# Small constants ahead of the weights, scan rows 521 wide, a pad at SBUF's right end: every large tile at a multiple of 256 bytes

## The chip, the cores and the metric

One core of a Trainium2 chip runs one decoder layer. The metric is device time of one execution, in microseconds (us), lower is better. The kernel before was timed in three runs: 2541.51, 2540.04 and 2535.76 us, median 2540.04. One more execution was recorded by the hardware profiler.

Engines: PE is TensorE (matmuls), PEld its load of the stationary operand, DVE is VectorE, ACT ScalarE, POOL GpSimd, SP the engine that issues most DMAs. SBUF is the working memory, 128 partitions wide; PSUM takes what PE writes.

## The reference

A layer for 2048 tokens of width 1024, in float32:

```
a = rmsnorm(x);  u = a @ W_in                       # 1024 x 2560
conv = swish(layernorm(depthwise_conv31(val * sigmoid(gate))))   # 512 channels
attn = per head: A[t,s] = sigmoid(z_ts) * prod_{s<j<t} (1 - sigmoid(z_tj)),  out = A @ v
h = x + rmsnorm(concat(conv, rmsnorm(attn)) @ W_out)
out = h + rmsnorm((silu(f @ W_gate) * (f @ W_up)) @ W_down),  f = rmsnorm(h),  hidden 2816
```

The attention has 8 heads of 64, no softmax: the product over the keys between is a running product, swept in blocks.

## The kernel before, in words

**Products.** Each float32 matrix product is made of three PE products in the type fp32r: every operand is split in a rounded part H and a rest L, and L·H, H·H and H·L are summed in PSUM. A PE product has a stationary operand of 128x128 (512 bytes a partition, loaded for every product by an instruction of its own) and a moving operand of 128x512 (2048 bytes a partition). In the names of the profile, `out<-moving,stationary`. `dense` (L251 to L260) is this for the input projection, `product` (L1017) for the block products of the feed-forward stage, `slot` (L1332) for the last product, both through the helper `matmul` (L763). There are also transposes: 128x128 products with the identity `idr` as the moving operand, such as L590.

**Stages.** A table (`PLAN`, L39) runs the input projections (L256 to L260), output projections (L689 to L691) and the first feed-forward products (names `c` and `p`) of four groups of 512 tokens one after the other. Beside them, at places that another table sets, run attention (`scores` L555, `values` L581), the 31 conv taps on DVE and sums of weights on POOL. When these are through (about 1520 us into the span) the feed-forward stage proper follows: `five` (L1099), a loop over 44 blocks of five products (names `b<-...`), and then the product with `w_down`, a loop over 154 `slots` (L1325; names `dps<-...`), which ends the kernel. On PE the order of both is written out in the program; it is not changed.

**Where tiles lie.** SBUF tiles come from pools. A pool takes the next free bytes of each partition from the left end (or, with `side="right"`, from the right end), in the order in which the pools are opened; a tile starts at a multiple of 32 bytes. So the place of every large tile follows from the sizes of the small ones that lie before it. The pools, from the left: `consts` (identity, vectors), `weights` (wH, wL, raw), `rows` (L145: rows of 1024, pieces of 512), `small` (L146: some 40 tiles of 4 to 64 bytes), `mixconsts` (L276: conv weights, layernorm vectors, mask), `acts` (L277: xH, xL), `sums`, `conv`, and then `attn` (L281: QH, QL, K, V, om, A, TH, TL) whose space the pool `late` (tiles e0 to e5) takes over in the feed-forward stage. From the right: `mixed` (L275), whose space `ffnt` (tiles t0 to t3) takes over. `om` (L567) holds a row of 512 factors and one more column, 513 in all, for the running product (L573).

Start addresses modulo 256, as the built programs have them:

| tiles | role on PE | before | after |
|---|---|---|---|
| idr | moving in transposes | 128 | 128 |
| wH, wL, and `a22h` in `rows` | stationary in most products, moving in the output projection | 64 | 0 |
| xH, xL | moving in most products; stationary in the output projection; both in `dps` | 192 | 0 |
| QH, QL, K, V | K moving, QH and QL stationary (L563, L564); V stationary (L595, L596) | 192 | 0 |
| A; TH, TL | stationary in transposes; moving (L595, L596) | 64 | 0 |
| e0 to e5 | moving in `five` | 192 | 0 |
| t0 to t3 | moving in `five` (second half) | 224 | 0 |
| om, four buffers | not read by PE | 192, 224, 0, 32 | 0, 64, 128, 192 |

PE reads slices of these tiles at steps of 512 or 2048 bytes, so a slice has the residue of its tile.

Of the kernel before, what the change touches and what calls it, by code (L numbers as in the profile page):

```python
# [9 lines left out]
F32 = mybir.dt.float32  # L10
# [8 lines left out]
P = 128  # L19
# [9 lines left out]
G = 512  # L29
# [6 lines left out]
NOM = 4  # L36
# [102 lines left out]
def layer_kernel(ctx: ExitStack, tc: tile.TileContext, x, xT, g_pre_mix, w_in, conv_w, conv_b, ln_g, ln_b,  # L139
                 attn_g, w_out, g_post_mix, g_pre_ffn, w_gate, w_up, w_down, g_post_ffn, out):  # L140
    nc = tc.nc
    cp = ctx.enter_context(tc.tile_pool(name="consts", bufs=1))
    dp = ctx.enter_context(tc.tile_pool(name="scratch", bufs=1, space=DRAM))
    wp = ctx.enter_context(tc.tile_pool(name="weights", bufs=2))
    rp = ctx.enter_context(tc.tile_pool(name="rows", bufs=3))  # L145
    sp = ctx.enter_context(tc.tile_pool(name="small", bufs=2))  # L146
    mm = ctx.enter_context(tc.tile_pool(name="mm", bufs=2, space=PSUM))

    idr = cp.tile([P, P], F32R, name="idr")
# [34 lines left out]
        nc.sync.dma_start(t, src.partition_broadcast(P))  # L184
        return t

    def rstd_of(dst, ss, n, tag="ms"):

        w = dst.shape[-1]
        m = sp.tile([P, 8], F32, tag=tag, name=tag, bufs=4)  # L190
        nc.gpsimd.tensor_scalar(m[:, 0:w], ss, 1.0 / n, EPS, ALU.mult, ALU.add)
        nc.gpsimd.tensor_tensor(dst, m[:, 0:w], nhalf[:, 0:w], ALU.pow)

    def rms_of(dst, src, junk=None):

        ss = sp.tile([P, 1], F32, tag="ss", name="ss", bufs=4)
        nc.scalar.activation(ev("junk", BF16, D) if junk is None else junk, src, AF.Square, accum_out=ss)
        rstd_of(dst, ss, D)
# [73 lines left out]

    A = ExitStack()
    M = ExitStack()
    cm = M.enter_context(tc.tile_pool(name="mixed", bufs=1, side="right"))  # L275
    cc = ctx.enter_context(tc.tile_pool(name="mixconsts", bufs=1))  # L276
    xp = ctx.enter_context(tc.tile_pool(name="acts", bufs=1))  # L277
    C = ExitStack()
    fup = C.enter_context(tc.tile_pool(name="sums", bufs=1))
# [1 line left out]
    ap = A.enter_context(tc.tile_pool(name="attn", bufs=2))  # L281
# [201 lines left out]
    def convnorm(g, acc):  # L483

        for t in range(TT):
            ts_ = slice(t * P, (t + 1) * P)
            ps = pp.tile([P, G], F32, tag="cv", name="lps", bufs=1)
            for c in range(CB):
                nc.tensor.transpose(ps[:, c * P:(c + 1) * P], acc[:, c, ts_], id32)
            y = vp.tile([P, CH], F32, tag="cy", name="cy", bufs=1)  # L490
            nc.scalar.activation(y, ps, AF.Copy)
            st = sp.tile([P, 6], F32, tag="st", name="st")
            nc.vector.bn_stats(st, y)
            mv = sp.tile([P, 3], F32, tag="mv", name="mv")
            nc.vector.bn_aggr(mv[:, 0:2], st)
            rstd_of(mv[:, 2:3], mv[:, 1:2], 1, "msc")
            nc.vector.scalar_tensor_tensor(y, y, mv[:, 0:1], lng, ALU.subtract, ALU.mult)
            nc.vector.scalar_tensor_tensor(y, y, mv[:, 2:3], lnb, ALU.mult, ALU.add)
            s = vp.tile([P, CH], F32, tag="cs", name="cs", bufs=1)
            nc.scalar.activation(s, y, AF.Sigmoid)  # L500
            nc.gpsimd.tensor_tensor(s, y, s, ALU.mult)
            for _ in range(LAG):
                yield 3
            pt = pp.tile([P, G], F32, tag="cv", name="cps", bufs=1).rearrange("p (c t) -> p c t", c=CB)
            for c in range(CB):
                nc.tensor.transpose(pt[:, c, :], s[:, c * P:(c + 1) * P], id32)
            r = s.rearrange("p (c t) -> p c t", c=CB)
            nc.scalar.activation(r, pt, AF.Copy)
            nc.scalar.dma_start(conv[g][:, :, ts_], r)
        done.add(("conv", g))  # L510
# [23 lines left out]
    def attn(g):  # L534
# [20 lines left out]
        def scores(u, j):  # L555
            hd_ = heads[u["h"]]
            diag = u["c"] == g
            w = (j + 1) * P if diag else G
            K = u["K"]
            z = pp.tile([P, G], F32, tag="z", name="z")  # L560
            late = g == NG - 1 and u["h"] >= NH // 2
            js = slice(j * P, (j + 1) * P)
            nc.tensor.matmul(z[:, 0:w], hd_["QL"][:, js], K[:, 0:w], start=True, stop=False)  # L563
            nc.tensor.matmul(z[:, 0:w], hd_["QH"][:, js], K[:, 0:w], start=False, stop=True)  # L564
            if diag:
                nc.vector.tensor_tensor(z[:, w - P:w], z[:, w - P:w], msk, ALU.add)  # L566
            om = ap.tile([P, G + 1], F32, tag="om", name="om", bufs=NOM)  # L567
            nc.gpsimd.tensor_copy(om[:, G:G + 1], hd_["prev"][j])
            nc.scalar.activation(om[:, G - w:G], z[:, 0:w], AF.Sigmoid, scale=-0.125)  # L569
            a = ap.tile([P, G], F32, tag="A", name="A", bufs=NA)  # L570
            nc.scalar.activation(a[:, 0:w], z[:, 0:w], AF.Sigmoid, scale=0.125)  # L571
            r = om[:, G - w:G + 1][:, ::-1]
            nc.vector.tensor_tensor_scan(r, r, (one if late else z[:, 0:1]).to_broadcast([P, w + 1]), one, ALU.mult, ALU.bypass)  # L573
            nc.gpsimd.tensor_tensor(a[:, 0:w], a[:, 0:w], om[:, G - w + 1:G + 1], ALU.mult)  # L574
            pv = sp.tile([P, 1], F32, tag="pv", name="pv", bufs=8)
            nc.gpsimd.tensor_copy(pv, om[:, G - w:G - w + 1])
            hd_["prev"][j] = pv
            u["A"].append(a)
            return w
# [295 lines left out]
    def input_sums(g, k, tmp, banks=bank, t4=None):  # L875

        def turn(k, name):
            ps = banks(name)
            for t in range(TT):
                nc.tensor.transpose(ps[:, t * P:(t + 1) * P], rows["h", (g + 1) * TT + t][:, k * P:(k + 1) * P], id32)  # L880
            return ps

        def piece(k, i):
            t = ev("piece")
            nc.sync.dma_start(t, stored["fx", g, k, i])
            return t

        def halves(n, t):
            if n == 4 and t4:
                sums_split(t4, k, t)  # L890
            else:
                part(t, k, TT, "B", g, n)

        lo, hi = gpf[:, k:k + 1], gpf[:, k + 4:k + 5]
        t1, b22, t3, t2 = tmp
        p12, p22 = turn(k, "b12"), turn(k + 4, "b22")
        b11, b21 = piece(k, 0), piece(k, 1)
        nc.scalar.activation(b22, p22, AF.Copy, scale=hi)
        yield
        nc.vector.scalar_tensor_tensor(t1, p12, lo, b11, mult, sub)  # L900
        nc.vector.scalar_tensor_tensor(t3, p12, lo, b22, mult, sub)
        nc.gpsimd.tensor_tensor(t1, t1, b21, sub)
        halves(3, b22)
        halves(7, t3)
        yield
        nc.gpsimd.tensor_tensor(t2, b22, t1, sub)
        halves(5, t1)
        halves(6, t2)
        t, b21 = piece(k + 4, 0), piece(k + 4, 1)
        yield  # L910
        nc.vector.tensor_tensor(t, t, t2, sub)
        nc.vector.tensor_tensor(t, t, b21, add)
        halves(4, t)
        yield
# [39 lines left out]
    for name, g, cost, *mid in PLAN:  # L954
# [14 lines left out]
        n = 0  # L969
# [15 lines left out]
    with ExitStack() as E:  # L985
# [247 lines left out]
        def steps():  # L1233
# [10 lines left out]
            for k in range(TT):  # L1244
                yield from input_sums(last, k, tmp, bank, B[last][4])
            M.close()
            R.append(ctx.enter_context(tc.tile_pool(name="ffnt", bufs=1, side="right", reuse_waits="tile")))
# [40 lines left out]
        ss = {}  # L1288
# [8 lines left out]
        def scale_of(T, c):  # L1297

            if c:
                return scales.pop(T)  # L1300
            ms = sp.tile([P, 1], F32, tag="msf", name="msf", bufs=4)
            g, q = T // (2 * TT), T % (2 * TT)
            nc.gpsimd.tensor_scalar(ms, ss[g][:, 0, q:q + 1], ss[g][:, 1, q:q + 1], EPS, add, add)  # L1303
            rs = sp.tile([P, 1], F32, tag="rs", name="rs", bufs=4)
            nc.gpsimd.tensor_tensor(rs, ms, nhalf[:, 0:1], ALU.pow)  # L1305
            scales[T] = rs
            return rs
# [3 lines left out]
        def finish(T, r, t, c):  # L1311
            rs = scale_of(T, c)
            cs_ = slice(c * G, (c + 1) * G)
            tc.keep_in_program_order(
                nc.vector.scalar_tensor_tensor(r[:, cs_], t, rs, r[:, cs_], mult, add))
# [131 lines left out]
```

## Time and profile before

| | |
|---|---|
| timed runs, median | 2540.04 us (2535.76 to 2541.51) |
| span of the profiled execution, first to last instruction | 2537.7 us |
| busy: PE, DVE, POOL, ACT | 95%, 71%, 60%, 51% |
| mean granted PE clock | 0.983 |
| DMA, mean | 259 GB/s |

The record lists no other time of the profiled execution; its span lies inside the range of the three runs. PE's busy time is an envelope: a 128x512 product is listed with some 390 ns from its start to its modelled end, but the next one starts well before that end. How fast PE goes is therefore read from the spacing of starts: the number of products in a stretch in which PE never stops. Each row of the view by stretches gives, for every engine, its busy time and in brackets its number of instructions.

### The profile page before, as it was taken

How to read it: one execution, taken by the hardware profiler on the slowest of the kernel's cores; microseconds unless marked ns; L12 is line 12 of the kernel's file. 1: busy time of each engine (PE TensorE's matmuls, PEld its weight loads, DVE VectorE, ACT ScalarE, POOL GpSimd, SP SyncE). 2: the span in 40 equal slices, each digit the busy share in tenths (PEclk: the TensorE clock that was granted, in tenths of full speed). 3: DMA queues.
4: the chain of work that ended last, by engine and by line, in shares of the span. 5: the costliest groups of instructions: out<-in, count | busy, mean ns of one | idle time of the engine just before them, and what ended most of it. 6: DMA issues, size and time to landing. Idle time of an engine off the chain costs nothing. (4 is left out here: it accounts for less than half of the span.)

```text
span 2537.7 us, 35647 instructions
## 1 busy us (share of the span) xinstructions
PE 2417.8 (95%) x11156; PEld 1952.5 (77%) x11156; DVE 1806.6 (71%) x2321; ACT 1292.9 (51%) x2398; POOL 1518.9 (60%) x1844
## 2 busy tenths in 40 slices
PE   7989989998899999999989999999999999999998
PEld 6878767776677877888778877777788888887886
DVE  5787579887899787777887536776666665557656
ACT  4554655646565565666667645332332224444443
POOL 5754678646563376646745408764665665558656
PEclk9989999999899999999999999999999999999999
DMA  9979987987576699765786686977878768667765
GB/s 346 318 271 320 298 256 257 366 273 253 180 269 218 193 305 335 242 229 187 242 279 216 217 293 226 342 277 244 306 276 274 261 224 300 196 194 262 251 188 178
DMA packets 289181, 657.31 MB, mean 259 GB/s; under 512 B 33888, under 2 KB 42080, under 8 KB 288992
## 3 DMA queue, kind: packets, MB, share of 16 engines
q1 hardware_dynamic: 264704, 622.01, 73.6%
q10 hardware_dynamic: 24288, 33.04, 3.6%
q8 instruction: 88, 1.44, 0.2%
q14 instruction: 101, 0.83, 0.1%
HBM read 460.92 MB, written 193.99 MB: 258 GB/s over the span
## 5 line engine op out<-in xcount | busy, mean ns | idle before, releaser
L574 POOL TENSOR_TENSOR A<-A,om 128x512 f32<-128x512 f32 (+2 forms) x320 | 320.5, 1003 | 322.1 <-DVE om L573 242.9
L1054 POOL TENSOR_TENSOR wL<-raw,wH 128x512 fp32r<-128x512 f32 x176 | 255.7, 1477 | 204.9 <-ACT wH L1053 197.1
L476 DVE SCALAR_TENSOR_TENSOR cv<-glu,cw,cv 128x512 f32<-128x512 f32 x464 | 346.5, 747 | 5.7
L573 DVE TENSOR_TENSOR_SCAN om<-om,one,z 128x513 f32<-128x513 f32 (+3 forms) x256 | 277.5, 1097 | 73.9 <-ACT A L571 65.5
L1285 DVE TENSOR_TENSOR xL__22005<-t__22007,xH__22004 128x512 fp32r<-128x512 f32 x154 | 198.9, 1297 | 158.7 <-ACT xH__22004 L1284 158.4
L1283 POOL TENSOR_TENSOR xL__22003<-t__22006,xH__22002 128x512 fp32r<-128x512 f32 x154 | 212.4, 1386 | 154.3 <-ACT xH__22002 L1282 151.9
L256 PE MATMUL inps<-xH,wL 128*128 128x512 f32 x640 | 262.1, 410 | 6.7 <-ACT sg L422 5.0
L569 ACT ACTIVATE om<-z 128x512 f32<-128x512 f32 (+2 forms) x320 | 171.6, 537 | 181.2 <-DVE z L566 76.0
L258 PE MATMUL inps<-xH,wH 128*128 128x512 f32 x640 | 258.4, 404 | 0.0
L260 PE MATMUL inps<-xL,wH 128*128 128x512 f32 x640 | 258.3, 405 | 0.0
L249 DVE TENSOR_TENSOR TL<-at,TH 128x512 fp32r<-128x512 f32 (+1 forms) x320 | 189.0, 598 | 92.6 <-ACT TH L248 91.7
L763 PE MATMUL dps<-xH__22002,xL__22005 128*128 128x512 f32 x616 | 240.3, 390 | 2.8 <-DVE xL__22005 L1285 1.5
L763 PE MATMUL dps<-xL__22003,xH__22004 128*128 128x512 f32 x616 | 240.2, 390 | 1.0 <-POOL xL__22003 L1283 1.0
L763 PE MATMUL dps<-xH__22002,xH__22004 128*128 128x512 f32 x616 | 239.8, 389 | 0.0
L248 ACT ACTIVATE TH<-at 128x512 fp32r<-128x512 f32 (+1 forms) x320 | 167.6, 545 | 86.8 <-PE at L590 84.0
L1282 ACT ACTIVATE xH__22002<-t__22006 128x512 fp32r<-128x512 f32 x154 | 97.2, 631 | 215.4 <-POOL xL__22003 L1283 121.8
L590 PE MATMUL at<-idr,A 128*128 128x128 f32 x1088 | 189.5, 278 | 5.7 <-POOL A L574 4.7
L210 ACT ACTIVATE wH<-raw 128x1024 fp32r<-128x1024 f32 x156 | 165.6, 1063 | 41.7 <-DMA raw<-in_w_in_dram 24.4
L571 ACT ACTIVATE A<-z 128x512 f32<-128x512 f32 (+2 forms) x320 | 167.8, 539 | 33.3 <-PE at L590 33.3
L1053 ACT ACTIVATE wH<-raw 128x512 fp32r<-128x512 f32 x176 | 101.2, 623 | 153.7 <-PE b L763 51.0
L590 PEld LDWEIGHTS at<-idr,A 128*128 128x128 f32 x1088 | 140.6, 143 | 43.3 <-POOL A L574 6.6
L847 POOL TENSOR_TENSOR sum<-sum 128x512 f32<-128x512 f32 x88 | 114.2, 1297 | 84.7 <-DMA sum<-in_w_up_dram 37.8
(303 smaller groups left out, 6378.9 us busy)
## 6 DMA issues: line engine op xcount, KB each, us to landing
wL<-wL SPq DMA_DIRECT2D x156, 512.0 KB, 4.8
raw<-in_w_in_dram SPq DMA_DIRECT2D x80, 512.0 KB, 6.0
t__22007<-u SPq DMA_DIRECT2D x154, 256.0 KB, 3.0
c<-c ACTq DMA_DIRECT2D x88, 256.0 KB, 4.2
t__22006<-wd SPq DMA_DIRECT2D x88, 256.0 KB, 3.0
K<-kd SPq DMA_DIRECT2D x80, 256.0 KB, 4.7
V<-vd SPq DMA_DIRECT2D x80, 256.0 KB, 4.1
u<-accf SPq DMA_DIRECT2D x22, 768.0 KB, 4.2
```

The source lines that it names most:

```text
L249: nc.vector.tensor_tensor(L, ps, H.bitcast(F32), ALU.subtract)
L256: nc.tensor.matmul(ps, WL[:, kc], aH[t](k), start=k == 0, stop=False)
L258: nc.tensor.matmul(ps, WH[:, kc], aH[t](k), start=False, stop=False)
L260: nc.tensor.matmul(ps, WH[:, kc], aL[t](k), start=False, stop=k == KT - 1)
L476: nc.vector.scalar_tensor_tensor(to, gl[c][:, k:k + G], cw[:, c, k:k + 1], a, ALU.mult, ALU.add))
L573: nc.vector.tensor_tensor_scan(r, r, (one if late else z[:, 0:1]).to_broadcast([P, w + 1]), one, ALU.mult, ALU.bypass)
L574: nc.gpsimd.tensor_tensor(a[:, 0:w], a[:, 0:w], om[:, G - w + 1:G + 1], ALU.mult)
L590: nc.tensor.transpose(pt[:, j * P:(j + 1) * P], u["A"][j][:, b * P:(b + 1) * P], id32)
L763: return nc.tensor.matmul(ps, a, b, skip_group_check=True, **flags)
L1054: nc.gpsimd.tensor_tensor(l, t, f32(h), sub)
L1283: nc.gpsimd.tensor_tensor(WL, w, f32(WH), sub)
L1285: nc.vector.tensor_tensor(UL, t, f32(UH), sub)
```

## The change

Four things are done to places in SBUF, and nothing to what is computed. The pools `mixconsts` and `small` are opened ahead of `weights`. A tile `edge` of 224 bytes is put at the right end, and POOL clears it. `om` is 521 columns wide instead of 513. Two tags of small tiles are made smaller: `msc` has two buffers instead of four, and the tile `msf` of the last stage takes over the buffers of `msa`, which the attention used.

```diff
     cp = ctx.enter_context(tc.tile_pool(name="consts", bufs=1))
     dp = ctx.enter_context(tc.tile_pool(name="scratch", bufs=1, space=DRAM))
+    cc = ctx.enter_context(tc.tile_pool(name="mixconsts", bufs=1))
+    sp = ctx.enter_context(tc.tile_pool(name="small", bufs=2))
     wp = ctx.enter_context(tc.tile_pool(name="weights", bufs=2))
     rp = ctx.enter_context(tc.tile_pool(name="rows", bufs=3))
-    sp = ctx.enter_context(tc.tile_pool(name="small", bufs=2))
...
-    def rstd_of(dst, ss, n, tag="ms"):
+    def rstd_of(dst, ss, n, tag="ms", bufs=4):
...
-        m = sp.tile([P, 8], F32, tag=tag, name=tag, bufs=4)
+        m = sp.tile([P, 8], F32, tag=tag, name=tag, bufs=bufs)
...
+    edge = ctx.enter_context(tc.tile_pool(name="edge", bufs=1, side="right"))
+    nc.gpsimd.memset(edge.tile([P, 56], F32, name="edge"), 0.0)
     cm = M.enter_context(tc.tile_pool(name="mixed", bufs=1, side="right"))
-    cc = ctx.enter_context(tc.tile_pool(name="mixconsts", bufs=1))
...
-            rstd_of(mv[:, 2:3], mv[:, 1:2], 1, "msc")
+            rstd_of(mv[:, 2:3], mv[:, 1:2], 1, "msc", 2)
...
-            om = ap.tile([P, G + 1], F32, tag="om", name="om", bufs=NOM)
+            om = ap.tile([P, G + 9], F32, tag="om", name="om", bufs=NOM)
...
-            ms = sp.tile([P, 1], F32, tag="msf", name="msf", bufs=4)
+            ms = sp.tile([P, 1], F32, tag="msa", name="msf", bufs=4)
```

On PE, DVE, ACT and SP both programs have the same instructions in the same order, with the same waits on the same engines. POOL has one instruction more. Its start, before (the first row is the constant -0.5, then identity, mask, ones and the conv's margins):

```order
L152 MEMSET nhalf 128x8
masks.py:197 MEMSET ident 128x128
L294 MEMSET msk 128x128
L298 MEMSET one 128x1
L303 MEMSET glu_132 128x30
```

and after:

```order
L153 MEMSET nhalf 128x8
L277 MEMSET edge 128x56
masks.py:197 MEMSET ident 128x128
L296 MEMSET msk 128x128
L300 MEMSET one 128x1
L305 MEMSET glu_137 128x30
```

Only the row of `edge` is new; the line numbers behind it are shifted, and every wait on a count of POOL's instructions counts one more.

## The prediction

> **What bounds the kernel now.** I read the page's busy times first. PE is busy almost throughout, at nearly its full granted clock:
>
> ```profile
> PE 2417.8 (95%) x11156; PEld 1952.5 (77%) x11156; DVE 1806.6 (71%) x2321; ACT 1292.9 (51%) x2398; POOL 1518.9 (60%) x1844
> PEclk9989999999899999999999999999999999999999
> ```
>
> Then the view by stretches, cut at the stages: projections with attention, the first part of `five`, its rest, a stretch inside `dps`, all of `dps`. The columns are busy us and number of instructions of PE, PEld, DVE, ACT and POOL, then granted clock, DMA share and GB/s.
>
> ```profile
> 0.00:1520.00 1520.00, 1429.82 (x6877) 1151.11 (x6878) 1154.52 (x1643) 895.42 (x1678) 870.38 (x1364) 0.98 0.80 265
> 1520.00:1800.00 280.00, 263.85 (x1133) 210.73 (x1133) 198.41 (x228) 106.43 (x184) 183.32 (x136) 0.99 0.80 277
> 1800.00:2100.00 300.00, 300.00 (x1290) 242.43 (x1289) 190.88 (x214) 87.11 (x153) 195.32 (x135) 1.00 0.77 266
> 2130.00:2290.00 160.00, 160.00 (x707) 132.52 (x706) 87.80 (x76) 79.58 (x151) 95.24 (x73) 1.00 0.63 197
> 2110.00:2537.70 427.70, 414.15 (x1817) 339.98 (x1815) 254.42 (x227) 199.46 (x376) 267.57 (x209) 0.99 0.68 220
> ```
>
> In the third and fourth rows PE never stops, at clock 1.00. These stretches hold products of one size only (128x512), so length over count is the time that PE takes for one: 300.00/1290 = 232.6 ns in `five`, 160.00/707 = 226.3 ns in `dps`. The chain that ended last says the same of two unbroken pieces that both lie on it:
>
> ```profile
> 1795.08 282.67 PE b L763 x1212
> 2125.56 158.07 PE dps L763 x696
> ```
>
> Without the 0.39 us in which the last one drains, (282.67 - 0.39)/1211 = 233.1 ns, and (158.07 - 0.39)/695 = 226.9 ns. **The same instruction costs 6.2 ns, 2.7%, more in one stage than in the next.** That difference is what this change turns on. The timeline of PE shows it arise where one stage passes into the other, without a pause (start, duration, out<-moving,stationary):
>
> ```profile
> 2102.02 0.40 PE L763 MATMUL b<-e__19607,wL 128*128 128x512 f32 x1
> 2102.26 0.40 PE L763 MATMUL b<-e__19607,wH 128*128 128x512 f32 x1
> 2102.49 0.40 PE L763 MATMUL b<-e__19608,wH 128*128 128x512 f32 x1
> 2102.73 0.39 PE L763 MATMUL dps<-xH__22002,xL__22005 128*128 128x512 f32 x1
> ...
> 2103.65 0.39 PE L763 MATMUL dps<-xH__22002,xH__22004 128*128 128x512 f32 x1
> 2103.88 0.39 PE L763 MATMUL dps<-xL__22003,xH__22004 128*128 128x512 f32 x1
> 2104.10 0.39 PE L763 MATMUL dps<-xH__22002,xL__22005 128*128 128x512 f32 x1
> ...
> 2104.78 0.39 PE L763 MATMUL dps<-xH__22002,xL__22005 128*128 128x512 f32 x1
> ```
>
> From 2102.73 to 2103.65, four products, the spacing is still 230 ns; from 2103.88 to 2104.78, four products, it is 225 ns. DMA, clock and the other engines do not switch within half a microsecond. What switches is the pair of operands: `five` reads tiles at residues 192 (e) and 64 (wH, wL) modulo 256, `dps` reads both operands from xH and xL, all at 192.
>
> **What each part of the change does.** I take the cause to be the distance between the moving stream and the load of the next stationary tile, modulo 256: unlike residues make them collide, like residues let them fall into step after some four products. More rows speak for it:
>
> ```profile
> L763 PE MATMUL b<-t__19202,wL 128*128 128x512 f32 x88 | 35.1, 398 | 0.0
> L763 PE MATMUL b<-t__19203,wH 128*128 128x512 f32 x88 | 34.7, 394 | 0.0
> L763 PE MATMUL b<-e__19608,wH 128*128 128x512 f32 x88 | 34.9, 396 | 0.0
> L763 PE MATMUL b<-e__19540,wL 128*128 128x512 f32 x88 | 34.6, 393 | 0.0
> L763 PE MATMUL dps<-xH__22002,xH__22004 128*128 128x512 f32 x616 | 239.8, 389 | 0.0
> L763 PEld LDWEIGHTS b<-e__19607,wH 128*128 128x128 f32 x88 | 16.6, 189 | 3.9
> L763 PEld LDWEIGHTS dps<-xH__22002,xH__22004 128*128 128x128 f32 x616 | 115.7, 188 | 23.8
> ```
>
> The tiles t (224 with 64) give products of 394 to 398 ns, the tiles e (192 with 64) 393 to 396, the like pair of `dps` 389: the two unlike pairs differ little, the like one stands apart. The loads themselves take 188 to 189 ns in both stages, so neither stream alone is slow. After the change all of these operands have residue 0, the like pair. I price a product in an unbroken run at the 226.9 ns of `dps`, the first four after a break at what they cost now.
>
> *Rest of `five`.* From 1795.08 to 2102.73 there are 307.65 us / 233.1 ns = 1,320 products; 1,320 x 6.2 ns = 8.2 us. All of it lies on the path: PE never stops there, and DVE is busy 64%, POOL 65%, ACT 29% of that stretch, DMA 77%; so they can feed a PE 2.7% faster. I take all of it.
>
> *First part of `five`.* 1,133 products at some 5.7 ns (all pairs 192 with 64) are 6.4 us. PE stands still here thirteen times:
>
> ```profile
> PE b L763 <- DVE cy L1061: 5.8, 4, 2.1
> PE b L763 <- POOL wL L1054: 4.2, 1, 4.2
> PE b L763 <- DVE glu L1061: 3.1, 4, 1.4
> PE b L763 <- DVE cs L1061: 3.0, 3, 1.7
> ```
>
> These are waits for an eviction (L1061) that starts when an earlier product of the same block ends, with another product of 12 matmuls between. Only what these 12 gain, of the 48 in a block here, is handed to the wait; so three quarters stay: 4.8 us.
>
> *Projections and attention.* The counts and the longest waits:
>
> ```profile
> L256 PE MATMUL inps<-xH,wL 128*128 128x512 f32 x640 | 262.1, 410 | 6.7 <-ACT sg L422 5.0 <-DMA wL<-wL 1.7
> L763 PE MATMUL c<-xH,wL 128*128 128x512 f32 x352 | 143.0, 406 | 0.1
> L689 PE MATMUL ops<-wH,xL 128*128 128x512 f32 x224 | 93.3, 417 | 7.5 <-DVE xL L527 4.7 <-DVE big L694 2.4 <-ACT big L696 0.3
> L763 PE MATMUL p<-xH,wL 128*128 128x512 f32 x88 | 35.5, 403 | 0.0
> L595 PE MATMUL o<-TH,V 128*128 128x512 f32 (+1 forms) x320 | 125.2, 391 | 9.1 <-ACT TH L248 5.5 <-ACT oT L660 3.1 <-DMA QL<-qd 0.2
> L590 PE MATMUL at<-idr,A 128*128 128x128 f32 x1088 | 189.5, 278 | 5.7 <-POOL A L574 4.7 <-ACT ma L630 0.5 <-DVE ot L612 0.4
> ...
> PE z L563 <- DVE om L573: 17.3, 27, 2.4
> PE o L596 <- DVE TL L249: 15.9, 16, 2.1
> ```
>
> The first four rows have two sister lines each: 3 x (640 + 352 + 224 + 88) = 3,912 products with unlike residues, and some 450 of `o`. The 320 calls that L595 counts each bring up to four transposes (L590), whose moving operand `idr` stays at residue 128: some 320 breaks, each of which costs four products their gain. That leaves about 3,000 x 5.7 ns = 17 us. PE is idle here for 90 of 1520 us, most of it behind the loop of the running product and the splits, where DVE is 76% busy and DMA 80%; a faster PE comes to these waits earlier and stands longer. Between nothing and 17 us I take 10, nearer the upper end, because PE is 94% busy.
>
> *`dps`* has like residues already: 0. *Transposes*: `idr` stays at 128 and A goes from 64 to 0, an unlike pair before and after: 0. *The `om` rows* lie on four residues before, and DVE does not care: in 40 us with eight full-width scans, two for each of the four buffers, their durations stay together:
>
> ```profile
> L573 DVE TENSOR_TENSOR_SCAN om<-om,one,z x11: 478/1274/1282, 999.4 to 1037.2; 128x513 f32<-128x513 f32 x8, 128x129 f32<-128x129 f32 x1, 128x257 f32<-128x257 f32 x1, 128x385 f32<-128x385 f32 x1
> ```
>
> The longest is 1282 ns and the median 1274. So I give the change nothing on DVE, ACT and POOL. *The clearing of `edge`*, 56 columns once, lies on POOL before anything waits for it: below 0.3 us. *Fewer buffers of `msc` and `msf`*: written and read by POOL alone, in order; no wait is added.
>
> Sum: 8.2 + 4.8 + 10 = 23.0 us. Against the span of the profiled execution, 2537.7 - 23.0 = 2514.7; that span is 2.3 us below the median, so against the median **2517 us**. Bounds of the known terms: 8.2 + 4.8 with nothing from the first stage gives 2527; everything that unlike products could give, 8.2 + 6.4 + 4,360 x 5.7 ns = 39 us, gives 2501.
>
> **The rivals.** *No change, 2540.* `dps` differs from `five` in more than residues: its moving tiles are reused for four banks, and PSUM banks change every third product, not every twelfth. If that makes the 226.9 ns, moving tiles gains nothing. For it: `z` (L563, L564) also has like residues, and its runs are too short to show a gain. Against it: the reuse of operands is much the same in both (two of three neighbours share one), and nothing in the timeline waits for a bank. [...]
>
> *Slower, 2551.* The spacing depends on the absolute place, and 192 is a good one, 0 an ordinary one. Then `five` stays at 233 and `dps` falls back to it: 3 x 616 products x 6.2 ns = 11.5 us lost. It would be decided in the first ten products of `dps`. Against it: the loads of tiles at 64 and at 192 take the same 188 to 189 ns, so no row shows the place of one operand to count alone.
>
> *Faster still, about 2480.* Like residues remove the collision, but a slice of 512 bytes that starts at 192 touches three blocks of 256 bytes, at 0 two. If such blocks count and 0 gives a second step as large as the first, `dps` gains 11 us and the other 6,800 products again what they gained, some 25: 2517 - 36 = 2481. No row shows it. [...]
>
> **How the numbers follow.** Forecast 74% (2501 to 2530), no change 11%, slower 7%, faster still 8%. The range 2497 to 2541 holds the forecast and most of no change, and leaves out the other two: about 8 in 10. A difference below 0.2%, 5 us, cannot be told from none; by the cases faster has 82%, the same 11%, slower 7%.
>
> **What would show it.** In the profile of the changed kernel the pieces of `five` without a pause should have 1,320 products in about 299.5 us (227 ns each) instead of 307.7, `dps` the same 227; PE's products by name should all come near 389 ns; the waits for L1061 and L573 should grow by a few us. Wrong would be: `five` still at 232 (no change), `dps` above 230 (the absolute place), both clearly below 226 (a second step), or `five` at 227 with the total unmoved, the gain then lying in longer waits.

## The result, and the profile after

The changed kernel took **2524.91 us** (median of 7 runs, 2521.93 to 2533.45), the kernel before 2540.82 us beside it (7 runs, 2535.76 to 2546.56). The ratio is 0.9945, with a 95% interval of 0.993 to 0.996: 10 to 18 us faster. The profiled execution took 2525.87 us with a span of 2523.9 us.

The page of the changed kernel, its span and busy times:

```profile
span 2523.9 us, 35648 instructions
PE 2392.2 (95%) x11156; PEld 1951.2 (77%) x11156; DVE 1796.9 (71%) x2321; ACT 1291.7 (51%) x2398; POOL 1522.1 (60%) x1845
```

PE is busy 25.6 us less (2417.8 before), with as many instructions; the loads (PEld) and ACT take what they took. The view by stretches, with the windows of the prediction but for the third, which here ends before `dps` begins:

```profile
0.00:1520.00 1520.00, 1423.02 (x6913) 1155.93 (x6914) 1152.50 (x1645) 898.56 (x1686) 876.50 (x1368) 0.97 0.79 266
1520.00:1800.00 280.00, 261.40 (x1145) 212.05 (x1144) 204.28 (x233) 106.49 (x184) 190.81 (x140) 0.99 0.83 290
1800.00:2060.00 260.00, 260.00 (x1148) 215.36 (x1148) 164.16 (x190) 76.83 (x135) 166.96 (x116) 1.00 0.78 269
2130.00:2290.00 160.00, 159.69 (x704) 131.77 (x703) 91.38 (x79) 76.43 (x145) 99.49 (x78) 1.00 0.62 196
```

The third row is `five` without a pause: 260.00/1148 = 226.5 ns a product, where it was 232.6. The fourth is `dps`: 159.69/704 = 226.8 ns, where it was 226.3. The timeline at the passage from the one stage to the other, where the spacing used to change:

```profile
2083.15 0.39 PE L765 MATMUL b<-e__19612,wL 128*128 128x512 f32 x1
...
2083.60 0.39 PE L765 MATMUL b<-e__19613,wH 128*128 128x512 f32 x1
2083.83 0.39 PE L765 MATMUL dps<-xH__22007,xL__22010 128*128 128x512 f32 x1
...
2084.96 0.39 PE L765 MATMUL dps<-xL__22008,xH__22009 128*128 128x512 f32 x1
```

Two spacings from the first row to the second, 0.45 us; five from the third to the last, 1.13 us: 226 ns on both sides. What PE waits for in the first stage and in `five` (us, times, longest), two rows and four:

```profile
PE o L598 <- DVE TL L250: 22.5, 20, 5.5
PE z L565 <- DVE om L575: 18.3, 30, 2.4
...
PE b L765 <- DVE cy L1063: 6.7, 4, 2.2
PE b L765 <- POOL wL L1056: 4.3, 1, 4.3
PE b L765 <- DVE glu L1063: 4.0, 4, 1.6
PE b L765 <- DVE cs L1063: 3.6, 3, 1.9
```

TL 22.5 for 15.9, om 18.3 for 17.3; in `five` the four rows sum to 18.6 for 16.1. So some of the gain has gone into waits. DVE's busy time is hardly shorter (1796.9 us for 1806.6), and the group of the scan, whose rows now start elsewhere, has the mean it had, 1097 ns. The products of `five` come to 389 to 391 ns by name, as the prediction asked, but for those at a wait or right behind it (395 to 405).

By stages, in the two profiled executions (starts of the first product of a stage, from the timelines):

| us | before | after | |
|---|---|---|---|
| to the first product of `five` | 1525.4 | 1517.2 | -8.2 |
| `five`, first part | 269.7 | 267.2 | -2.5 |
| `five`, rest | 307.6 | 299.4 | -8.2 |
| `dps`, to the end | 435.0 | 440.1 | +5.1 |
| span | 2537.7 | 2523.9 | -13.8 |

The last stage, for which nothing was forecast, is **5.1 us longer**, at an unchanged spacing. The waits of PE in it, before:

```profile
PE dps L763 <- DVE xL__22005 L1285: 1.5, 2, 0.9
PE dps L763 <- ACT t__22009 L1356: 1.3, 1, 1.3
```

and after:

```profile
PE dps L765 <- DVE xL__22010 L1287: 4.5, 2, 3.9
...
PE dps L765 <- ACT t__22014 L1358: 0.6, 1, 0.6
```

One wait of 3.9 us stands where one of 0.9 us was. The chain that ended there (start, duration, what):

```profile
2083.77 6.27 DMA e__22019<-hd
...
2090.11 7.85 DMA e__22017<-hd
...
2098.03 10.10 DMA t__22012<-u
...
2109.64 30.49 PE dps L765 x121
```

At 2083.77, when the last product of `five` sets the e tiles free, eight loads of `hd` (512 KB each) begin to be issued into them. The fetches of the next slots' operands (`t<-u`, 256 KB) share the transfers with them (from 2084 to 2108 us the DMA share is 1.01, at 378 GB/s), and one takes 10.1 us. PE arrives after 96 products and stands. The chain before has the same three transfers, and a wait of only 0.9 us behind them:

```profile
2101.78 5.54 DMA e__22014<-hd
...
2107.39 7.58 DMA e__22012<-hd
...
2115.03 9.02 DMA t__22007<-u
...
2125.56 34.52 PE dps L763 x151
```

Measured from the first product of `dps` (2102.73 before, 2083.83 after), PE comes to this place no earlier than before: its 96th product starts after 21.5 us in both. It is the fetch that lands later, after 24.3 us instead of 21.3. The three transfers take 2.1 us more, and the first of them is issued 0.9 us later in the stage. And the pause has a second price, in the timeline after:

```profile
2105.36 0.39 PE L765 MATMUL dps<-xL__22008,xH__22009 128*128 128x512 f32 x1
2109.64 0.80 PE L765 MATMUL dps<-xH__22007,xL__22010 128*128 128x512 f32 x1 [3.89 <-DVE xL__22010 L1287]
...
2110.66 0.63 PE L765 MATMUL dps<-xL__22008,xH__22009 128*128 128x512 f32 x1
...
2114.93 0.63 PE L765 MATMUL dps<-xH__22007,xL__22010 128*128 128x512 f32 x1
```

From 2110.66 to 2114.93 are ten products of 427 ns: for 6 us after the pause PE runs at half its clock (granted: 0.50 from 2110 to 2115), some 13 products that cost 0.2 us too much each, 2.6 us. The pause is 3.0 us longer than before, and before there is no such slow stretch behind it: 3.0 + 2.6, less 0.7 for the wait for `t`, is 4.9 of the 5.1 us.

### The profile page after: what moved, and what is told of

It reads as the page before. It is cut to its first block, busy times and chain, and to the rows that moved or that the text cites. A ratio compares the mean times of both kernels' runs of the same rounds, so it can differ in the third digit from the quotient of the medians.

```text
span 2523.9 us, 35648 instructions
## 1 busy us (share of the span) xinstructions
PE 2392.2 (95%) x11156; PEld 1951.2 (77%) x11156; DVE 1796.9 (71%) x2321; ACT 1291.7 (51%) x2398; POOL 1522.1 (60%) x1845
## 5 line engine op out<-in xcount | busy, mean ns | idle before, releaser
L575 DVE TENSOR_TENSOR_SCAN om<-om,one,z 128x513 f32<-128x513 f32 (+3 forms) x256 | 277.5, 1097 | 70.9 <-ACT A L573 65.4
```

## Experiments

**Distance alone.** The theory: what counts is that moving and next stationary tile have like residues modulo 256, wherever that is. Rivals: the multiple of 256 itself is what helps, or it was something else that the change moves (order of pools, rows of 521). Three kernels make the distance unlike again, or the place another one, by a gap of some bytes; with it `edge` is made smaller by as much, so that the tiles on the right keep in step. All instructions and waits stay, but for one clearing by POOL. The first undoes the likeness with 128 bytes between the weights (at 0) and all other tiles (at 128), and keeps the rest of the change.

```diff
-    nc.gpsimd.memset(edge.tile([P, 56], F32, name="edge"), 0.0)
+    nc.gpsimd.memset(edge.tile([P, 24], F32, name="edge"), 0.0)
+    gap = ctx.enter_context(tc.tile_pool(name="gap", bufs=1))
+    nc.gpsimd.memset(gap.tile([P, 32], F32, name="gap"), 0.0)
     xp = ctx.enter_context(tc.tile_pool(name="acts", bufs=1))
```

> The changed kernel with one tile of 128 bytes put between the pools rows and acts, and the right end's pad shortened from 224 to 96 bytes: wH, wL, a22h stay at residue 0, all other large tiles stand at 128. Same instructions in the same order. Theory (the distance of the moving tile to the next stationary one, modulo 256, decides): a product of five and of the projections is unlike again, as before the change: the rest of five at 232 to 233 ns a product, dps (both operands at 128) at 226.9, time 2536 to 2541 us. Rival (the absolute place decides: multiples of 256 are good): five slow too, but dps falls to 230 to 233 as well, time 2548 us or more. Rival (the order of pools or the width of om brought the gain, not residues): 2525 us, five at 227.

Measured: 2538.83 us, ratio 0.9995 (0.9983 to 1.0007) to the kernel before: the whole gain is gone. The unbroken piece of `five` that the prediction reads, in the chain of this kernel:

```profile
1794.40 281.94 PE b L767 x1212
```

(281.94 - 0.39)/1211 = 232.5 ns. `dps`, whose pair stays alike at 128, keeps 226.9.

The second moves all tiles together to residue 64, with a gap ahead of the weights:

```diff
-    nc.gpsimd.memset(edge.tile([P, 56], F32, name="edge"), 0.0)
+    nc.gpsimd.memset(edge.tile([P, 40], F32, name="edge"), 0.0)
+    gap = ctx.enter_context(tc.tile_pool(name="gap", bufs=1))
+    nc.gpsimd.memset(gap.tile([P, 16], F32, name="gap"), 0.0)
     wp = ctx.enter_context(tc.tile_pool(name="weights", bufs=2))
```

> The changed kernel with 64 bytes put ahead of the pool weights and the right end's pad shortened by 64: every large tile at residue 64, none at a multiple of 256. Theory (only the distance counts): as the changed kernel, five and dps at 226.7 to 227.2 ns, time 2522 to 2528 us. Rival (the start at a multiple of 256 counts): five at 230 to 233 ns, time 2536 us or more.

Measured: 2521.35 us, ratio 0.9931 (0.9916 to 0.9946), `five` at (275.17 - 0.39)/1211 = 226.9 ns:

```profile
1780.66 275.17 PE b L767 x1212
```

So the multiple of 256 is not needed, and the pools' order and the rows are not what helps. The changed kernel itself ran beside the two:

> The changed kernel itself, once more, as the control of this call. Time 2525 us. Its profile showed dps standing still for 5 us near its start, behind the loads of hd; before the change that was 1.3 us. Theory (chance of DMA: the burst of loads takes some us more or less): this time between 0 and 6 us, not always more than before. Rival (five ends earlier and the burst does not): 4 us or more again, in every profile of this call with a fast five.

Measured: 2526.04 us, ratio 0.9951 (0.9933 to 0.9969); (299.67 - 0.39)/1319 = 226.9 ns in `five`:

```profile
1785.39 299.67 PE b L765 x1320
```

The wait near the start of `dps` is 2.5 us here, 2.1 us in the kernel shifted by 64 and 1.6 us in the one with the gap of 128, so the rival (4 us or more each time) fell: the 3.9 us of the first profile were a long one.

**The transposes.** `idr` is still unlike to A after the change, and the groups of transposes might break the step of the products around them. In this kernel `idr` is taken from its pool after three small tiles, and so lies at residue 0:

```diff
-    idr = cp.tile([P, P], F32R, name="idr")
-    id32 = idr.bitcast(F32)
...
     gpm = const(cp, "gpm", g_pre_mix, [P, KT])
+    idr = cp.tile([P, P], F32R, name="idr")
+    id32 = idr.bitcast(F32)
```

(`rstd2`, another small tile of the pool, moves with it.)

> The changed kernel with idr moved behind three small tiles, from residue 128 to 0: now every tile that PE reads stands at a multiple of 256. Same instructions, same order. Theory (a transpose's spacing follows its load, and the few products behind a break need some four products to fall into step whatever idr's place): 2525 us, within 4 us of the changed kernel; transposes at 109 ns. Rival (the identity at 128 throws the streams out of step at each of some 320 breaks): 4 to 6 us faster, the products of the projections nearer to 227 ns.

Measured: 2523.66 us, ratio 0.9945 (0.9926 to 0.9965), not to be told from the changed kernel; the products of the input projection are spaced 228.5 ns on average, 228.7 without the edit. The residue of `idr` is worth nothing that can be seen. The transposes have a median spacing of 109 ns with and without the edit.

**How far apart.** The prediction took all unlike distances for alike. The same gap as in the first kernel with 32, 64 and 192 bytes (`gap` of 8, 16 and 48 columns, `edge` of 48, 40 and 8) tells whether they are.

> As the run with 128 bytes between the pools rows and acts, with 32: weights at residue 0, all other large tiles at 32. Theory (any unlike distance makes the streams collide, as 128 and 160 did before): five at 231 to 234 ns a product, dps at 226.9. Rival (the collision grows with the distance, as of two windows that overlap): five between 227 and 230 ns.

> The same with 64 bytes: weights at 0, the rest at 64. Theory (any unlike distance): five at 231 to 234 ns, dps at 226.9. Rival (grows with the distance): five at 228 to 231 ns. Rival (the period is 64 bytes and not 256, and 128 is unlike only by chance of the order): five at 227.

> The same with 192 bytes: weights at 0, the rest at 192, so the moving tile stands 64 bytes below the next multiple. Theory (any unlike distance): five at 231 to 234 ns. Rival (the sign counts, the stream that is ahead wins): five here and in the run with 64 bytes differ by more than 2 ns.

One run each: 2550.94, 2532.8 and 2534.51 us. For `five` the first gives (267.90 - 0.39)/1146 = 233.4 ns in a piece cut by the window,

```profile
1802.25 267.90 PE b L767 x1147
```

the second (277.79 - 0.39)/1211 = 229.1 ns,

```profile
1791.21 277.79 PE b L767 x1212
```

and the third (283.07 - 0.39)/1211 = 233.4 ns:

```profile
1791.48 283.07 PE b L767 x1212
```

So the theory that all unlike distances are alike fell: 64 loses a third of what the others lose. The loss doesn't grow with the distance either, and the period isn't 64 bytes. And the sign counts. In `ops` the weights move and the other tiles (x, and the tiles e of this stage) are stationary, so 64 and 192 change places. Nine spacings of the second kernel (gap of 64):

```profile
1503.11 0.39 PE L693 MATMUL ops<-wH,e__17079 128*128 128x512 f32 x1
...
1505.21 0.40 PE L695 MATMUL ops<-wL,e__17078 128*128 128x512 f32 x1
```

2.10 us / 9 = 233 ns; eight of the third (gap of 192):

```profile
1501.29 0.39 PE L694 MATMUL ops<-wH,e__17078 128*128 128x512 f32 x1
...
1503.12 0.40 PE L695 MATMUL ops<-wL,e__17078 128*128 128x512 f32 x1
```

1.83 us / 8 = 229 ns. Over all unbroken pairs of `ops` the means are 233.3 and 229.9, against 229.0 and 233.3 in `five`. In both, moving minus stationary of 64 is the cheaper one. The 2550.94 us of the first kernel is more than its spacing explains (as slow as the third's, 16 us apart in one run each); 10.8 of the 16 us arise before `five`, which it reaches at 1531.0 us (the third at 1520.1), and 5.2 in `dps`, where its trace has a wait of 2.1 us for xL and one of 1.8 us for `t`. Its mean granted clock was 0.979, the third's 0.983; what lies behind the 10.8 us is not shown.

**The loads of hd.** The theory for the 5.1 us in `dps`: the eight loads stand in the way of the fetches. The rival: something in `dps` became slower. In this kernel each load is issued only after the latest fetch of the slots:

```diff
+        fetched = [None]
...
-            nc.sync.dma_start(t, stored["u3", g, j][:, (5, 6, 3).index(n), :] if n in (5, 6, 3) else stored["u", g, n, j])
+            fetched[0] = nc.sync.dma_start(t, stored["u3", g, j][:, (5, 6, 3).index(n), :] if n in (5, 6, 3) else stored["u", g, n, j])
...
-                nc.sync.dma_start(r, hd[T])
+                with tc.issue_after(fetched[0].ins):
+                    nc.sync.dma_start(r, hd[T])
```

> The changed kernel with the eight loads of hd in the last stage issued on SP behind the fetch of the slot at which they are written, instead of 30 slots earlier at the start of dps. Theory (the pause at the start of dps comes from the fetches of slots that queue behind 4 MB of hd): the first pause of dps falls from 2.3 to 4.3 us to below 1 us, dps from 425 to 430 us to 423 to 425, time 2 to 4 us less than the changed kernel, 2521 to 2523 us. Rival (the fetches are late for another reason, or the loads of hd collide later): dps as long as before, time 2523 to 2527 us.

Measured: **2517.71 us**, ratio 0.9916 (0.9895 to 0.9938) to the kernel before. What PE waits for in the whole of `dps`:

```profile
PE dps L765 <- POOL xL__22008 L1287: 1.5, 3, 0.6
PE dps L765 <- DVE xL__22010 L1289: 0.6, 1, 0.6
```

The pause is gone, and the first 842 products of `dps` run without a wait; the time lies below the 2521 to 2523 us expected. In the 29 us from the end of `five` a fetch `t<-u` lands in a median of 4.6 us, where the changed kernel has 6.5 and the kernel before 5.8:

```profile
t__22012<-u SPq DMA_DIRECT2D x13, 256.0 KB, 4.6
```

Then the same edit on the kernel before, and the pair of both edits once more beside it:

> The kernel before, its tiles where they were, with the loads of hd issued only after the fetch that is one slot away. Theory (the first pause of dps is there because fetches queue behind the hd loads, and it grew only because PE comes to it earlier): before has 1.1 us of this pause, so the edit gives 1 to 4 us, dps takes 421 to 424 us against 424.9, time 2536 to 2539. Rival (the edit helps by something else in dps, a flat 5 us): 2535 or less with the first pause unchanged.

> The changed kernel with the same edit of the hd loads, beside the kernel before with it, on one chip. Theory (like residues give some 8 us before five and 11 in five, and without the loads in the way nothing is lost in dps): 18 to 21 us below the kernel before with the same edit, 2515 to 2520. Rival (part of the gain is lost at the end whatever the loads do): 14 us or less below it.

Measured: 2536.09 us, ratio 0.9988 (0.9975 to 1.0001), and 2521.73 us, 0.9933 (0.9917 to 0.9948). From the first to the last product `dps` takes 422.3 us in both, as in the run above (422.1); with the loads as they were it takes 424.9 before and 430.0 after. So with the loads out of the way the two layouts end alike, and the loss in `dps` was the loads' doing. That the pause grew because PE comes to it earlier, as the expectation has it, is not what the traces show (21.5 us after the first product in both). Between the two medians lie 14.4 us, below the 18 to 21 that the theory expected and nearer to its rival, while the spans of the two profiled executions lie 23.0 us apart (2539.0 and 2516.0). With intervals of 3 and 4 us to each side of the two ratios this pair does not settle how large the gain is without the loads; the stages below do it better.

## Why the prediction was right, and where its steps were off

Taken together, the profiles with unlike tiles (before, the gap of 128, the late loads on the kernel before) reach `five` at 1525.4, 1524.7 and 1528.2 us, those with like tiles (six) at 1514.2 to 1518.8 us: means 1526.1 and 1516.0. `five` takes 577.1 to 577.7 us in the ones, 566.2 to 567.2 in the others.

- **The cause, distance modulo 256: right.** A gap of 128 bytes alone takes the whole gain back; a common shift by 64 keeps it. That refutes *no change* (reuse of operands, PSUM banks) and *slower* (the absolute place): `dps` is at 226.9 ns at residues 192, 0, 128 and 64. *Faster still* fell too: no pair is clearly below 226.
- **Rest of `five`: 8.2 forecast, 8.2 measured**, at the 226.9 ns taken over from `dps`.
- **First stage: 10 forecast, 8.2 in the profiled pair, 10.1 in the means.** The 10 was chosen between 0 and 17, so that it came out is partly luck, and its working was rougher than that. The first four products after a break were to keep their cost and the later ones to have the full gain; averaged over the unbroken runs of the first stage (spacings below 250 ns), products 1 to 4 have 231.6 ns (231.8 before the change), 5 to 8 229.2 (233.1), 9 to 12 227.6 (232.3), the later ones 226.7 (232.5). So the first four do keep their cost, but it takes eight to twelve products until the full gain is there, as in this run of the changed kernel, which begins with two products of `z` at 532.00 and 532.31:

```profile
532.55 0.40 PE L259 MATMUL inps<-xH,wH 128*128 128x512 f32 x1
...
534.17 0.39 PE L261 MATMUL inps<-xL,wH 128*128 128x512 f32 x1
...
536.44 0.39 PE L257 MATMUL inps<-xH,wL 128*128 128x512 f32 x1
```

  (Seven spacings to the second row, 1.62 us / 7 = 231 ns; ten from there, 2.27 us / 10 = 227.) Waits took the part expected of them (TL 6.6 us more).
- **First part of `five`: 4.8 forecast, 2.5 measured. This is the term that was mis-sized.** The step "an eviction that starts when an earlier product of the same block ends, with another product of 12 matmuls between" was wrong. The chain of the kernel before at such a wait:

```profile
1699.91 3.50 PE b L763 x15
...
1703.44 0.71 DVE b L1061
...
1707.66 0.69 DVE cs L1061
...
1711.75 0.61 DVE cs L1061
...
1712.41 2.59 PE b L763 x10
```

  From the end of a product at 1703.41 to PE's next start lie 9.0 us of DVE's chain, in which PE does some 34 products and then waits 1 us. What these 34 gain is handed to the wait, 34 of 96 products instead of a quarter. The pauses themselves say so: where they recur every 96 products (four in a row from 1712 us on), the break between two products is 1.04 us before and 1.24 after, so 0.20 of the 0.52 us that 96 products gain are lost again. That takes 38%, and 6.4 us becomes 4.0. The four rows of waits, 2.5 us more in sum, say the same (6.4 - 2.5 = 3.9); the last 1.4 us I have not traced. (The prediction's rows count twelve waits, not thirteen.)
- **`dps`: 0 forecast, 5.1 lost in the profiled pair, 1.8 in the means** (425.6 us with unlike tiles, 427.4 over four like profiles with the loads of `hd` as they were). The step was "like residues already: 0". It looked at the spacing alone, and not at the fetches at the start of the stage, which share the transfers with the loads of `hd` and had been hidden before but for a wait of 0.9 us. That the loads cause the pause is shown by holding them back; why it grew is not. At this place PE waits 0.9 and 1.6 us in the two unlike profiles with the loads as they were, 3.9, 2.5, 2.1 and 2.3 us in the four like ones, but also 2.1, 2.4 and 0.8 us with the gaps of 32, 64 and 192, though PE's 96th product starts 21.5 to 21.7 us into the stage in all of them. The chain quoted in the prediction for `dps` starts right behind that pause, at 2125.56, where PE had waited 0.9 us.
- **The sum: 23.0 forecast; 13.8 in the profiled pair, 15.9 between the medians.** The stages' means give 10.1 + 10.8 - 1.8 = 19.1, the mean spans of the two unlike and the four like profiles with the loads of `hd` as they were 17.9. Rest of `five` is right, and the first stage by its size; 2.3 us are the eviction chain, 2 to 5 the pause in `dps`.

## What to carry to other kernels

Where a stage of equal products runs without a pause, divide its length by its count, and compare with another stage: 2.7% between two stages with equal instructions was a matter of where tiles start, and moving their starts got it back. Place the tiles that are loaded and those that stream at equal addresses modulo 256; which address was of no account at the four tried (`dps` has 226.9 ns a product with both operands at 0, 64, 128 or 192). This is shown for fp32r products of 128x512 with a load each, and for nothing else. And when an engine at the bound gets faster, follow it into the stages that the change seems not to touch: here a wait for a fetch went from 0.9 to 3.9 us in the profiled pair, and its stage from 435.0 to 440.1 us at an unchanged spacing. Putting eight loads behind the fetches brought `dps` down to 422.1 to 422.3 us, from 424.9 before the change and 430.0 after it. In the whole time its worth is not settled: 2517.71 and 2521.73 us in two measurements against 2524.91 and 2526.04 of the changed kernel, but 2521.35 in the kernel shifted by 64, without that edit, and the intervals overlap.

## What was not expected of the hardware

- The spacing of 128x512 products, each with its own load, by the start of the moving tile minus that of the next stationary one, modulo 256: 226.7 to 226.9 ns at 0, 233.4 at 32, 229.0 at 64, 232.5 at 128 (233.1 before the change, where a part of the tiles was at 160), 233.4 at 192; for 64 and 192 the sign is shown by `ops`. The loads' own time, 188 to 189 ns, is the same in both stages of the kernel before; but the spacing is not (233.1 and 226.9 ns), and it follows the two starts together, so by these traces the load and the running product do affect each other. Where they meet, no run here shows.
- After some pauses PE runs at half its rate for a few microseconds: 427 ns a product for 6 us after 3.9 us of idling. Shorter pauses sufficed too: in `dps` it does so after 2.5 us in the repeated run of the changed kernel and after 2.3 us with `idr` moved (mean granted clock 0.83 in the 10 us around each), not after 2.1 us in the kernel shifted by 64 (1.00). Nor does the length of the pause alone decide: in the kernel with the gap of 32 bytes PE goes on at its full rate after 2.06 us, and at half of it (0.42 us from product to product) after 1.81 us:

```profile
2134.68 0.50 PE L767 MATMUL dps<-xH__22012,xL__22015 128*128 128x512 f32 x1 [2.06 <-DVE xL__22015 L1289]
2135.02 0.40 PE L767 MATMUL dps<-xH__22012,xH__22014 128*128 128x512 f32 x1
2135.25 0.40 PE L767 MATMUL dps<-xL__22013,xH__22014 128*128 128x512 f32 x1
...
2355.78 0.50 PE L767 MATMUL dps<-xH__22012,xL__22015 128*128 128x512 f32 x1 [1.81 <-ACT t__22019 L1360]
...
2356.80 0.63 PE L767 MATMUL dps<-xH__22012,xL__22015 128*128 128x512 f32 x1
2357.22 0.63 PE L767 MATMUL dps<-xH__22012,xH__22014 128*128 128x512 f32 x1
```

  So a pause of 2.1 to 2.5 us can cost 1.6 us more (in the 10 us around the pauses of 2.5 and 2.3 us PE does 26 and 27 products in 7.46 and 7.74 us, which take 5.9 and 6.1 us at 226.9 ns each), or nothing (35 products in 7.87 us around the one of 2.1 us); this is part of why the profiles of the four like kernels with the loads of `hd` as they were differ by 8 us (2516.1 to 2523.9).
- The mean granted clock was 0.9837 over 70 runs with unlike tiles and 0.9820 over 31 with like ones (those of the experiments with several runs each), and runs with a clock higher by 0.001 were 1.6 us shorter. If the lower clock is a consequence of the faster products, it eats by my estimate 2.7 us of the gain (1.7 times 1.6 us). That is a correlation; no run tests it.
